# Low parts of weights and norms all subtracted on VectorE instead of every third on GpSimd

## The chip, the cores and the metric

The kernel runs on one core of a Trainium2 chip. Its five engines work in their own order each and wait for each other through semaphores: TensorE (PE in the profile, with its weight load as PEld), VectorE (DVE), ScalarE (ACT), GpSimd (POOL) and SyncE (SP), which here issues the loads. The metric is the device time of one execution in microseconds (us); less is better.

## The reference

The program chains two transformer blocks on a sequence of 256 tokens, width 1024, in fp32. Cut to what matters here:

```python
def first_block(x, ...):
    for layer in range(DEPTH):                       # DEPTH = 2
        h = rms_norm(x, norm1_g[layer])
        sb = cols(SB_OFF, SB_COLS)                   # cols: h @ w_in[layer][:, lo:lo + width]
        y_sb = merge_heads(stick_breaking_attention(...))
        y_rwkv, v_first = rwkv7_time_mix(cols(RWKV_OFF, RWKV_COLS), ...)
        y_moba = merge_heads(moba_attention(q_m, k_m, ...))
        y_hgrn = hgrn2_mixer(...)
        for n, y_n in enumerate((y_sb, y_rwkv, y_moba, y_hgrn)):
            gate = jax.nn.sigmoid(cols(GATE_OFF + n * D_MODEL, D_MODEL))
            term = gate * (y_n @ w_branch[layer, n])
            merged = term if merged is None else merged + term
        x = x + merged @ w_out[layer]
...
def second_block(x, c, ctx, ...):
    mod_l = jax.nn.silu(c) @ w_mod[l] + b_mod[l]
...
    out_c, out_l = mixer(h_c, h_l, ...)              # latent attention and an mLSTM
    x = x + g1[:, None, :] * out_l
    h_l = modulate(rmsnorm(x, norm2[l]), sh2, sc2)
    x = x + g2[:, None, :] * ec_moe(h_l, ...)        # 16 experts
    return rmsnorm(x, final_norm)
```

Behind the mixers each layer of the first block has a norm and an FFN of width 2816, silu(gate) * up, then down. All products are of fp32 quality.

## The kernel before, in words

**How a product is made.** TensorE gets fp32r operands (rounded fp32). To keep the precision, every operand is split into a high part (its copy to fp32r) and a low part (the operand minus that copy). `mm3` (L225) then runs three products into one accumulator: high x high (L227), high weight x low activation (L228) and low weight x high activation (L229), or with the sides exchanged in `proj_tok`.

**Weights.** A pair of halves (`weights`, L219) is the unit of work. `half_weights` (L205) loads one half, 128 x 1024 fp32 (512 KB), on SP's queue into tile wr (L214), ScalarE copies it into wh (`copy`, L179), and the subtraction wr - wh gives wl (`sub`, L182). The pools of wr, wh and wl have four buffers each. A counter `nsplit` sends every third half's subtraction (`NS = 3`, L1969) to GpSimd, the others to VectorE. 349 such halves or parts of halves are subtracted: 234 on VectorE, 115 on GpSimd.

**Norms.** `norm_split` (L335) scales x by the gain and the reciprocal root r (t, L191) and splits the result in high and low, block by block (eight blocks of 128 x 256). In the form without bias, the third and the sixth block's subtraction goes to GpSimd. r comes from a sum of squares (`square_sums` L272 or `rms` L301: products into sm at L280, L285, L309), a short chain of tiny VectorE instructions on tile nr (`rsqrt`, L259), and a spread over the partitions on TensorE (`spread`, L288, L291).

**Other work that the trace names.** VectorE's helpers record one line each: `sub` L182, `add` L185, `mul` L188, `stt` L191 (scalar_tensor_tensor), `ts` L194. In the FFN, `silu_mul` (L1072) makes of a pair of accumulators: u = gate * r, tanh on ScalarE (L1076), t = (t + 1) * u (L191, both inputs in SBUF), u = t * up (L188, `t<-t,acc`, one input in PSUM), u * r on GpSimd (L188, `t<-t,rr`), and the split into ff (L202 on ScalarE, L191 on VectorE, `r<-t,r`). Such GpSimd work that is no low part (the multiplications with rr, some squares and additions in the mixers, masks) is not touched by the change. The mixers run interleaved: `weave` (L867) draws from several streams of emitted work by a table of rates, and waits of TensorE in them carry their lines: L399 (rotation), L415 and L437 (MoBA attention), L642, L674 and L852 (the RWKV recurrence), L1646 (the mLSTM). `modulation` (L1130) loads w_mod in pieces on SP's queue (L1151) between the weight loads and multiplies them at L1155 into wm.

**Order.** The program emits tiles in the order of its loops and of `weave`; the framework's scheduler then fixes one order per engine. Where an instruction is given to another engine, neighbours can change place. The last part, from about 1467 us on, is the mixture of experts, whose weights come as 191 pieces of 1 MB on SP's queue (L1808), used at L1832 and behind.

Of the kernel before, what the change touches and what calls it, by code (L numbers as in the profile page):

```python
# [141 lines left out]
class Block:  # L142
    def __init__(self, ctx, tc, a, out):
        self.ctx, self.tc, self.a, self.out = ctx, tc, a, out
        nc = self.nc = tc.nc
        self.V, self.S, self.G, self.T = nc.vector, nc.scalar, nc.gpsimd, nc.tensor
        e = ctx.enter_context
        self.const = e(tc.tile_pool(name="const", bufs=1))
        self.ps = e(tc.tile_pool(name="ps", bufs=1, space=PSUM))
        self.per = e(tc.tile_pool(name="per", bufs=1))  # L150
        self.cst1 = self.cst2 = None
        self.nsplit = 0


    def C(self, name, lo=0, n=None):
# [49 lines left out]
    def half_weights(self, ap, parts=1):  # L205

        n = ap.shape[1]
        raw = self.wraw.tile([128, 1024], F32, tag="wr", name="wr")[:, 0:n]
        hi = self.whi.tile([128, 1024], F32R, tag="wh", name="wh")[:, 0:n]
        lo = self.wlo.tile([128, 1024], F32R, tag="wl", name="wl")[:, 0:n]  # L210
        self.nsplit += 1
        for i in range(parts):
            c = slice(i * n // parts, (i + 1) * n // parts)
            self.nc.sync.dma_start(raw[:, c], ap[:, c])  # L214
            self.copy(hi[:, c], raw[:, c])
            self.sub(lo[:, c], raw[:, c], hi[:, c], eng=self.G if self.nsplit % NS == 0 else self.V)
        return lambda c, w: (hi[:, c:c + w], lo[:, c:c + w])

    def weights(self, ap, n):  # L219
# [115 lines left out]
    def norm_split(self, x, nk, n, eps, gcol, hi, lo, bias=None, r=None):  # L335

        if r is None:
            r = self.rms8(x) if nk == 8 else self.rms([self.square(x[:, k]) for k in range(nk)], n, eps)
        for k in range(nk):
            h = self.t1()  # L340
            self.stt(h, x[:, k], gcol(k), r, ALU.mult, ALU.mult)
            if bias is None:
                self.split(hi[:, k], lo[:, k], h, eng=self.G if k % 3 == 2 else None)
            else:
                self.S.activation(hi[:, k], h, AF.Identity, bias=bias(k))
                self.stt(lo[:, k], h, bias(k), hi[:, k], ALU.add, ALU.subtract)
# [1619 lines left out]
SMB = 1  # L1966
BV = 1
MS = 0.13
NS = 3  # L1969
FN = 22.3  # L1970
IN = 4.0
GN = 8.2
# [101 lines left out]
```

## Time and profile before

| what | value |
|---|---|
| median of 3 runs | 1900.16 us (1897.15 to 1907.84) |
| the profiled execution | 1902.35 us |
| its span, first to last instruction | 1900.6 us |
| mean granted TensorE clock | 0.931 |
| PE busy | 1691.7 us (89%) |
| DVE busy | 915.7 us (48%) |
| ACT busy | 719.9 us (38%) |
| POOL busy | 454.2 us (24%) |
| read from HBM | 413.63 MB |

Busy times are those of the profiled execution. An engine that is busy is working on an instruction or is held inside one; the profile does not tell these apart. A wait is idle time of an engine, put down to the instruction that released it last. The granted clock is the share of full TensorE speed.

### The profile page before, as it was taken

The page shows a single profiled execution, that of the slowest core. Times are in us where ns is not written, and L with a number is a line of the kernel's source. Part 1 is how long each engine was busy: PE and PEld are TensorE (multiplying, and loading weights), DVE is VectorE, ACT ScalarE, POOL GpSimd, SP SyncE. Part 2 cuts the span into 40 slices and gives each one's busy share as a digit, 9 for nine tenths or more (in the row PEclk, how much of TensorE's full clock was granted, in tenths as well). Part 3 has the DMA queues.
Part 4 walks back from the last instruction along what each step waited for, and adds up shares of the span by engine and source line. Part 5 has one row for each costly group of instructions (what it writes and reads, how often), then busy time and mean ns, then how long its engine had stood idle before and what let it go on. Part 6 is the DMA issues. An engine that isn't in the chain of part 4 may idle for free. (4 is left out here: it accounts for less than half of the span.)

```text
span 1900.6 us, 34082 instructions
## 1 busy us (share of the span) xinstructions
PE 1691.7 (89%) x14380; PEld 1345.7 (71%) x14380; DVE 915.7 (48%) x1395; ACT 719.9 (38%) x1136; POOL 454.2 (24%) x285
## 2 busy tenths in 40 slices
PE   7899899999999799999999999989997976766665
PEld 7668799999989688997998998867896410201113
DVE  8755645577547765553776458453574100000001
ACT  5535544444446455543444444544443300000001
POOL 4352143244323622331443211111231000000000
PEclk9899999999999899999999999989999986767788
DMA  6552546455554235567554553321457999999997
GB/s 225 170 169 96 165 158 190 149 184 172 178 161 155 79 102 185 171 206 238 167 183 143 180 183 130 101 72 65 161 204 301 422 427 427 427 427 427 427 427 320
DMA packets 96378, 416.91 MB, mean 219 GB/s; under 512 B 10688, under 2 KB 12384, under 8 KB 71520
## 3 DMA queue, kind: packets, MB, share of 16 engines
q1 hardware_dynamic: 96224, 414.72, 60.1%
q8 instruction: 113, 1.85, 0.4%
q14 instruction: 41, 0.34, 0.1%
HBM read 413.63 MB, written 1.05 MB: 218 GB/s over the span
## 5 line engine op out<-in xcount | busy, mean ns | idle before, releaser
L227 PE MATMUL acc<-s,wh 128*128 128x256 f32 (+1 forms) x2236 | 652.3, 292 | 11.5 <-ACT wh L179 7.5
L228 PE MATMUL acc<-s,wh 128*128 128x256 f32 (+1 forms) x2236 | 648.0, 290 | 5.3 <-DVE s L191 4.0
L229 PE MATMUL acc<-s,wl 128*128 128x256 f32 (+1 forms) x2236 | 647.8, 290 | 0.4 <-DVE wl L182 0.4
L179 ACT ACTIVATE wh<-wr 128x1024 fp32r<-128x1024 f32 (+2 forms) x349 | 359.4, 1036 | 341.6 <-PE acc L228 201.0
L227 PEld LDWEIGHTS acc<-s,wh 128*128 128x128 f32 x2236 | 436.5, 195 | 28.1 <-issue 15.7
L228 PEld LDWEIGHTS acc<-s,wh 128*128 128x128 f32 x2236 | 436.8, 195 | 15.9 <-issue 7.9
L229 PEld LDWEIGHTS acc<-s,wl 128*128 128x128 f32 x2236 | 436.8, 195 | 4.3 <-issue 1.8
L182 POOL TENSOR_TENSOR wl<-wr,wh 128x1024 fp32r<-128x1024 f32 (+1 forms) x115 | 280.9, 2442 | 660.4 <-ACT wh L179 583.9
L182 DVE TENSOR_TENSOR wl<-wr,wh 128x1024 fp32r<-128x1024 f32 (+2 forms) x234 | 303.9, 1300 | 239.4 <-ACT wh L179 238.3
L1832 PE MATMUL mx<-s,s 128*32 128x512 f32 x640 | 111.7, 788 | 44.4 <-DMA s<-in_w_moe_dram 44.2
L1832 PEld LDWEIGHTS mx<-s,s 128*32 128x32 f32 x640 | 15.6, 121 | 124.4 <-DMA s<-in_w_moe_dram 113.9
L1832 PE MATMUL mx<-mw,s 128*32 128x512 f32 x384 | 68.3, 784 | 26.6 <-DMA mw<-in_w_moe_dram 26.5
L188 POOL TENSOR_TENSOR t<-t,rr 128x256 f32<-128x256 f32 x44 | 42.7, 971 | 127.4 <-DVE t L188 124.7
L1832 PEld LDWEIGHTS mx<-mw,s 128*32 128x32 f32 x384 | 8.8, 121 | 77.1 <-DMA mw<-in_w_moe_dram 67.2
L191 DVE SCALAR_TENSOR_TENSOR x<-acc,mod,x 128x256 f32<-128x256 f32 x28 | 12.2, 479 | 103.4 <-PE acc L1840 100.0
L188 DVE TENSOR_TENSOR m<-m,mx 128x1024 f32<-128x1024 f32 x4 | 4.9, 1221 | 112.0 <-PE mx L1832 112.0
L227 PE MATMUL mx<-r,wh 128*128 128x256 f32 x208 | 58.7, 282 | 0.0
L228 PE MATMUL mx<-r,wh 128*128 128x256 f32 x208 | 58.6, 282 | 0.0
L229 PE MATMUL mx<-r,wl 128*128 128x256 f32 x208 | 58.4, 281 | 0.0
L191 DVE SCALAR_TENSOR_TENSOR m<-m,mx 128x1024 f32<-128x1024 f32 x4 | 4.9, 1219 | 107.0 <-ACT m L1863 107.0
L191 DVE SCALAR_TENSOR_TENSOR t<-t,t 128x256 f32<-128x256 f32 (+1 forms) x46 | 46.8, 1016 | 12.3 <-ACT t L1076 8.2
L1832 PE MATMUL mx<-mw,ht 128*32 128x512 f32 x264 | 39.5, 704 | 14.5 <-DMA mw<-in_w_moe_dram 14.4
(516 smaller groups left out, 2526.5 us busy)
## 6 DMA issues: line engine op xcount, KB each, us to landing
s<-in_w_moe_dram SPq DMA_DIRECT2D x101, 1024.0 KB, 19.6
mw<-in_w_moe_dram SPq DMA_DIRECT2D x90, 1024.0 KB, 19.6
wr<-in_w_in_dram SPq DMA_DIRECT2D x158, 512.0 KB, 3.9
wr<-in_w_gu_dram SPq DMA_DIRECT2D x88, 512.0 KB, 4.3
wr<-in_w_down_dram SPq DMA_DIRECT2D x32, 512.0 KB, 4.3
wr<-in_w_out_dram SPq DMA_DIRECT2D x24, 512.0 KB, 3.8
qk<-in_w_mod_dram SPq DMA_DIRECT2D x32, 256.0 KB, 3.1
wr<-in_w_branch_dram SPq DMA_DIRECT2D x16, 512.0 KB, 4.2
```

The costliest lines, as they stand in the source:

```text
L179: self.S.activation(out, in_, AF.Copy)
L182: (eng or self.V).tensor_tensor(out, a, b, op=ALU.subtract)
L188: (eng or self.V).tensor_tensor(out, a, b, op=ALU.mult)
L191: self.V.scalar_tensor_tensor(out, a, s, b, op0=op0, op1=op1)
L227: T.matmul(out, wh, xh, start=start, stop=False)
L228: T.matmul(out, wh, xl, start=False, stop=False)
L229: T.matmul(out, wl, xh, start=False, stop=stop)
L1832: T.matmul(ps[32 * e:32 * e + 32], lhs(k, e), w[:, e * 512:(e + 1) * 512], start=k == 0, stop=k == 7, tile_position=(0, 32 * e))
```

## The change

`half_weights` gives every low part to VectorE, and `norm_split` as well; the counter and its constant are gone.

```diff
@@ -208,12 +207,11 @@
         lo = self.wlo.tile([128, 1024], F32R, tag="wl", name="wl")[:, 0:n]
-        self.nsplit += 1
         for i in range(parts):
             c = slice(i * n // parts, (i + 1) * n // parts)
             self.nc.sync.dma_start(raw[:, c], ap[:, c])
             self.copy(hi[:, c], raw[:, c])
-            self.sub(lo[:, c], raw[:, c], hi[:, c], eng=self.G if self.nsplit % NS == 0 else self.V)
+            self.sub(lo[:, c], raw[:, c], hi[:, c])
         return lambda c, w: (hi[:, c:c + w], lo[:, c:c + w])
...
@@ -340,7 +338,7 @@
             if bias is None:
-                self.split(hi[:, k], lo[:, k], h, eng=self.G if k % 3 == 2 else None)
+                self.split(hi[:, k], lo[:, k], h, eng=None)
...
-NS = 3
```

115 subtractions of weight halves and five of norms leave GpSimd's order and stand in VectorE's. Lines of the changed kernel are one smaller from L152 on and two smaller from about L211 on (L182 is L181 there, L191 is L190). On TensorE 139 of 11489 matmuls stand elsewhere than before, none by more than 60 places; on SP 7 of 668 instructions.

VectorE, the reciprocal root of the first layer's norm (nr), before:

```order
L194 TENSOR_SCALAR nr<-sm 128x2
L194 TENSOR_SCALAR nr<-nr 128x2
L188 TENSOR_TENSOR nr<-nr 128x2
L191 SCALAR_TENSOR_TENSOR nr<-nr 128x2 x2
L188 TENSOR_TENSOR nr<-nr 128x2 x2
L194 TENSOR_SCALAR nr<-nr 128x2
L191 SCALAR_TENSOR_TENSOR nr<-nr 128x2 x2
L182 TENSOR_TENSOR wl<-wr,wh 128x1024
L188 TENSOR_TENSOR qk<-acc,rr 128x512
```

The same place on VectorE in the changed kernel:

```order
L193 TENSOR_SCALAR nr<-sm 128x2
L181 TENSOR_TENSOR wl<-wr,wh 128x1024
L193 TENSOR_SCALAR nr<-nr 128x2
L187 TENSOR_TENSOR nr<-nr 128x2
L190 SCALAR_TENSOR_TENSOR nr<-nr 128x2
L181 TENSOR_TENSOR wl<-wr,wh 128x1024
L190 SCALAR_TENSOR_TENSOR nr<-nr 128x2
L187 TENSOR_TENSOR nr<-nr 128x2 x2
L193 TENSOR_SCALAR nr<-nr 128x2
L181 TENSOR_TENSOR wl<-wr,wh 128x1024
L190 SCALAR_TENSOR_TENSOR nr<-nr 128x2 x2
L181 TENSOR_TENSOR wl<-wr,wh 128x1024
L187 TENSOR_TENSOR qk<-acc,rr 128x512
```

Three weight subtractions moved from behind or beside the chain into it, so that four stand where one stood.

VectorE, two tiles of the first layer's FFN (t, r and acc as in `silu_mul`; the number is the tile's), before:

```order
L188 TENSOR_TENSOR t_4568<-t_4569,acc 128x256
L182 TENSOR_TENSOR wl<-wr,wh 128x1024
L191 SCALAR_TENSOR_TENSOR r_4071<-t_4568,r_4071 128x256
L188 TENSOR_TENSOR t_4638<-acc,rr 128x256
L191 SCALAR_TENSOR_TENSOR t_4639<-t_4639,t_4638 128x256
L188 TENSOR_TENSOR t_4638<-t_4639,acc 128x256
L191 SCALAR_TENSOR_TENSOR r_4072<-t_4638,r_4072 128x256
L182 TENSOR_TENSOR wl<-wr,wh 128x1024
```

The same place on VectorE in the changed kernel:

```order
L187 TENSOR_TENSOR t_4568<-t_4569,acc 128x256
L181 TENSOR_TENSOR wl<-wr,wh 128x1024
L190 SCALAR_TENSOR_TENSOR r_4071<-t_4568,r_4071 128x256
L187 TENSOR_TENSOR t_4638<-acc,rr 128x256
L181 TENSOR_TENSOR wl<-wr,wh 128x1024
L190 SCALAR_TENSOR_TENSOR t_4639<-t_4639,t_4638 128x256
L187 TENSOR_TENSOR t_4638<-t_4639,acc 128x256
L181 TENSOR_TENSOR wl<-wr,wh 128x1024
L190 SCALAR_TENSOR_TENSOR r_4072<-t_4638,r_4072 128x256
```

In the tile t_4638 one subtraction now stands between the first product and t = (t + 1) * u, and one between the last product and the low part r_4072.

## Rows read from the trace of the kernel before

**Rows 1.** Stretches: from:to, length, busy us (and instructions) by engine, clock, DMA share, GB/s.
```profile
0.00:1467.00 1467.00, 1383.85 (x12432) 1260.37 (x12436) 885.36 (x1334) 686.76 (x1066) 454.18 (x285) 0.97 0.50 162
1467.00:1900.00 433.00, 307.89 (x1952) 85.34 (x1944) 30.39 (x61) 33.16 (x71) 0.00 (x0) 0.79 0.98 412
600.00:650.00 50.00, 41.24 (x437) 35.79 (x435) 45.09 (x53) 29.55 (x48) 21.07 (x12) 0.92 0.35 115
```

**Rows 2.** The page's groups of weight subtractions: busy, mean ns | idle before, releaser.
```profile
L182 POOL TENSOR_TENSOR wl<-wr,wh 128x1024 fp32r<-128x1024 f32 (+1 forms) x115 | 280.9, 2442 | 660.4 <-ACT wh L179 583.9
L182 DVE TENSOR_TENSOR wl<-wr,wh 128x1024 fp32r<-128x1024 f32 (+2 forms) x234 | 303.9, 1300 | 239.4 <-ACT wh L179 238.3
```

**Rows 3.** Timeline, one FFN tile: start, us, engine, line, operation, [idle before <-releaser].
```profile
425.03 2.40 POOL L182 TENSOR_TENSOR wl<-wr,wh 128x1024 fp32r<-128x1024 f32 x1 [1.48 <-ACT wh L179]
425.34 2.37 DVE L191 SCALAR_TENSOR_TENSOR t<-t,t 128x256 f32<-128x256 f32 x1 [0.54 <-ACT t L1076]
428.31 0.36 PE L227 MATMUL acc<-s,wh 128*128 128x256 f32 x1 [0.35 <-DVE t L188]
```

**Rows 4.** Groups by shape of VectorE and GpSimd between 350 and 550 us (FFN).
```profile
L191 DVE SCALAR_TENSOR_TENSOR t<-t,t 128x256 f32<-128x256 f32 x22 | 23.0, 1044 | 4.1 <-ACT t L1076 4.1
L191 DVE SCALAR_TENSOR_TENSOR r<-t,r 128x256 fp32r<-128x256 f32 x13 | 12.5, 960 | 15.1 <-ACT r L202 15.1
L188 DVE TENSOR_TENSOR t<-t,acc 128x256 f32<-128x256 f32 x22 | 9.3, 421 | 0.8
...
L182 POOL TENSOR_TENSOR wl<-wr,wh 128x1024 fp32r<-128x1024 f32 x18 | 43.3, 2406 | 45.0 <-ACT wh L179 23.7 <-PE mx L229 19.9 <-PE acc L228 1.5
```

**Rows 5.** What TensorE waited for: us in total, times, longest us.
```profile
PE wm L1155 <- DMA qk<-in_w_mod_dram: 8.6, 3, 7.6
...
PE sm L642 <- DVE r L191: 4.0, 2, 2.5
PE acc L228 <- DVE s L191: 4.0, 2, 2.0
PE mx L437 <- DVE s L194: 3.6, 3, 3.0
...
PE acc L227 <- DVE t L188: 2.9, 8, 0.4
...
PE sm L309 <- DVE t L185: 2.7, 1, 2.7
PE sm L280 <- ACT t L278: 2.7, 1, 2.7
PE sm L309 <- DVE t L188: 2.5, 1, 2.5
...
PE mx L674 <- DVE s L518: 2.1, 1, 2.1
...
PE sm L399 <- ACT s L179: 1.4, 1, 1.4
...
PE acc L228 <- DVE s L182: 1.1, 1, 1.1
...
PE acc L229 <- DVE wl L182: 0.4, 1, 0.4
```

**Rows 6.** The first of eight stretches at low clock, and the sum of the eight.
```profile
17.00:23.80 6.80, 5.99 (x28) 5.99 (x29) 3.95 (x15) 0.89 (x2) 0.39 (x1) 0.50 0.44 139
...
sum 34.30, PE 33.49 PEld 27.35 DVE 18.62 ACT 7.76 POOL 3.58; mean PE 4.19 PEld 3.42 DVE 2.33 ACT 0.97 POOL 0.45
```

**Rows 7.** Timeline, first layer's mixers at 65 us: GpSimd and VectorE.
```profile
65.20 2.70 POOL L182 TENSOR_TENSOR wl<-wr,wh 128x1024 fp32r<-128x1024 f32 x1
...
66.20 2.25 DVE L182 TENSOR_TENSOR t<-t 128x512 f32<-128x512 f32 x1
```

**Rows 8.** Timeline at 175 us: GpSimd and VectorE.
```profile
175.20 2.36 POOL L182 TENSOR_TENSOR wl<-wr,wh 128x1024 fp32r<-128x1024 f32 x1
...
176.12 0.69 DVE L693 TENSOR_TENSOR am<-mx,cst 128x512 f32<-128x512 f32 x1 [0.44 <-PE mx L691]
```

More of the change, by code (lines that the diff above doesn't have):

```diff
@@ L151, in __init__ @@
         self.cst1 = self.cst2 = None
-        self.nsplit = 0
     def C(self, name, lo=0, n=None):
```

## The prediction

> **What bounds the kernel now.** I read the busy times in two stretches first. Up to 1467 us TensorE is busy for 1383.85 of 1467 us, so it stands still for about 83 us, and neither VectorE (885.36) nor GpSimd (454.18) is full. Behind 1467 us the DMA share is 0.98 at 412 GB/s, and VectorE is busy for 30.39 us, GpSimd for none [rows 1]. That tail is the loading of the experts' weights. It starts when the work before it ends, so a gain before 1467 us should arrive at the end of the program undiminished, and nothing is to be gained behind it.
>
> Second, the low-part subtractions themselves: 234 run on VectorE at 1.30 us, 115 on GpSimd at 2.44 us, and GpSimd waited 583.9 us in front of its own for ScalarE's high copy [rows 2]. So GpSimd has time to spare. What its subtractions cost has to be looked for elsewhere, in what VectorE does beside them.
>
> There it is seen in the timeline of one tile of the first layer's FFN. GpSimd subtracts from 425.03 on for 2.40 us. VectorE's t<-t,t starts at 425.34 and ends with it, after 2.37 us, and TensorE's next tile starts 0.35 us late [rows 3]. The groups of this stage show the pattern: t<-t,t, with both inputs in SBUF, takes 1044 ns on average, while t<-t,acc of the same size, with one input in PSUM, takes 421 [rows 4]. I read this as a hold: a VectorE instruction with two SBUF inputs does not move while a GpSimd subtraction runs.
>
> Third, what stands still because of it: the list of what TensorE waited for. The waits that I connect with a GpSimd subtraction are the two on s (L191), the longest ones of L642 and L437, the eight small ones of the FFN, L309 twice, L280, L674, and five of 1.1 to 1.4 us (L399, L1646, L415, L852 and L228 on L182; first and last are shown) [rows 5]. In each of them a subtraction of GpSimd lies in the chain that releases TensorE. The largest wait, 7.6 us on the load of w_mod, is the end of a load that was issued late, see below.
>
> **The change, part by part.**
>
> *Removed from GpSimd:* 115 weight subtractions, 280.9 us [rows 2], and five of the norms. GpSimd's busy time should fall from 454.18 to about 170.
>
> *Added to VectorE:* 115 x 1.30 + 5 x 0.42 = 152 us. *Given back to VectorE:* in the FFN stage 22 x (1.044 - 0.421) = 13.7 and 13 x (0.960 - 0.421) = 7.0, 20.7 us by 22 subtractions (18 and four narrower ones) [rows 4], or 0.94 each; by 115 of these some 108 us. VectorE's busy time, 915.8, should end between that and 960. So VectorE is about as full as before, with the idle time inside its instructions turned into work.
>
> *Term 1, stops that go.* A hold is worth at most what the row shows, 2.37 - 0.42 = about 2.0 us [rows 3, 4]. With this cap on each stop: L309 2.0 + 2.0, L228 on s 4.0, L642 2.0, L437 2.0, L227 2.9, L280 2.0, L674 2.0, the five small ones 6.2; together 25.1. In some of them something else is late next (ScalarE's own share of the chain, or a hold by one of the instructions that GpSimd keeps), so I take four fifths, **-20.1**. Bounds: 0 and -25.1.
>
> *Term 2, moved subtractions that land in front of something that TensorE waits for.* VectorE works in its order, and the order shows it: in the first norm's chain for the reciprocal root, four subtractions now stand where one stood at the end, so the 2 us that are gained there go back; in the FFN one more stands in every second or third tile between the product and the low part. No row of before prices this as a stop: TensorE's only wait on a wl of VectorE is 0.4 us [rows 5]. Lower bound 0, if all fall into VectorE's idle time. For the upper bound: the 24 stops of term 1 are ends of chains of some 5 us (an estimate; the FFN's piece of it takes 3 us, 425.34 to 428.31), 120 of 1467 us, or one in twelve. If the scheduler puts them where VectorE is busiest it could be one in five: 24 x 1.3 = +31. I take one in twelve of 120, 10 x 1.3, **+13.0**, since the stops are known places and the subtractions are spread like the weights.
>
> *Term 3, the clock.* [...] Most stops only get shorter, and other stops stay, so I take a third, **-5.7**. Bounds: 0 and -17.2.
>
> *Term 4, the late load.* VectorE's subtraction at 66.20 took 2.25 us beside a GpSimd subtraction of 2.70 that began at 65.20 [rows 7]; one of that size takes 0.69 where it is not held [rows 8]. Behind it on VectorE follows a weight subtraction that frees a raw buffer; behind that, on SP's queue, the weight load that needs the buffer, and behind that the w_mod load on which TensorE waits for 7.6 us [rows 5]. The chain starts 2.25 - 0.69 = 1.6 us earlier: **-1.6**. Bounds: 0, and -7.6 if the load gets through before it is needed.
>
> *Costed at nothing:* the weights' own lead. The raw, high and low pools hold four halves each. TensorE waited 0.4 us in all for a low part, so a subtraction that comes 1 or 2 us later or earlier is covered by the halves in hand; without that cover, each would cost its lateness. SP's queue keeps its order but for a few loads at the start that change place with a neighbour.
>
> Sum: -20.1 + 13.0 - 5.7 - 1.6 = **-14.4**. The profiled execution took 1902.35, so 1887.95; the median of the runs, 1900.16, is 2.2 lower, and I say **1887**.
>
> [...] At 176.12 VectorE's am<-mx,cst, with one input in PSUM, took its 0.69 us in the midst of a GpSimd subtraction of 2.36 us that began at 175.20 [rows 8]. [...] There the change buys nothing and only adds 1.3 us each. If all 115 were like this, VectorE would end at 915.8 + 152 = 1068 and term 1 would be nothing; rows 3 and 4 show that they are not.
>
> **The rivals.**
>
> *The insertions take it all back.* Condition: 27.4 us of gain divided by 1.3, 21 subtractions land in front of something TensorE needs, near the upper bound of term 2. For it: between 600 and 650 us VectorE is busy for 45.09 of 50 us [rows 1], with no idle place left. Against it: the hold costs VectorE 0.94 per subtraction and the work 1.3, so even there the engine's load hardly grows. Time: about 1900. [...]
>
> *Slower: subtractions that wait at the head of VectorE's queue.* GpSimd could afford to wait for the high copies, 583.9 us over 115, 5.1 each; VectorE waited 238.3 over 234, 1.0 each [rows 2]. What waits there now keeps the mixers' work behind it. Price: 1.3 + 1.0 = 2.3 for each that sits in front of a chain to TensorE. It decides from 27.4 / 2.3 = 12 of 120; with 18 of them the time is 1902 + 14, **1916**. For it: 83 us of idle TensorE are little, and every new stop may lower the clock too. Against it: the halves are fetched four ahead, so most copies are done early.
>
> *Larger gain.* The clock stays up behind all eight stops and the load comes in time: -20.1 + 13.0 - 17.2 - 7.6 = -31.9, **1870**. For it: clock and stop lie side by side in the rows. Against it: neither the stops nor VectorE's chains go away whole.
>
> That the change does not do what it says can be left out: no low part of a weight is left in GpSimd's order.
>
> **How the numbers follow.** Chances: forecast 0.50 (its own range 1878 to 1896), larger gain 0.12, taken back 0.18, slower 0.20. A measurement of this kernel can tell about 0.5%, 9.5 us, from no change: faster is below 1890.7, which takes seven tenths of the forecast's case and the larger gain, 0.47; the rest of the forecast and the case at 1900 make 0.33; slower 0.20. Range 1868 to 1911: the low end is the larger gain, the high end holds the first part of the slower case and the bound of term 2 (-20.1 + 31 = +11 without clock and load). Outside stay about 0.04 below and 0.12 above.
>
> **What would show it.** Right: POOL busy about 170 us and no wl among its groups; t<-t,t near 0.5 us where it was 1.044; L227 no longer waiting on the FFN's t; DVE busy between 916 and 960; waits on L309, L642, L228 shorter by up to 2 us each; fewer windows at clock 0.50. Wrong: new waits of TensorE on DVE wl or on chains with a wl in them, idle time of DVE before L181 well above 238 us, or TensorE's idle time up to the experts' weights not below 83 us. The tail behind it must stay as long as it is, 433 us; if it shrinks or grows, my account of its bound is wrong.

## The result

The changed kernel takes 1855.16 us (median of 4 runs, 1853.51 to 1857.60), the kernel before in the same comparison 1902.16: a ratio of 0.9753, 95% interval 0.9721 to 0.9785, or 47 us. Faster was forecast, but with 15 us; 1855 lies below the range.

The page of the changed kernel begins with the engines' busy times; of its groups I show the weight subtraction and the one multiplication of the FFN that stays on GpSimd.

```profile
PE 1671.1 (90%) x14380; PEld 1333.6 (72%) x14380; DVE 929.7 (50%) x1515; ACT 725.7 (39%) x1136; POOL 166.1 (9%) x165
...
L181 DVE TENSOR_TENSOR wl<-wr,wh 128x1024 fp32r<-128x1024 f32 (+2 forms) x349 | 425.9, 1222 | 324.3 <-ACT wh L178 323.2
...
L187 POOL TENSOR_TENSOR t<-t,rr 128x256 f32<-128x256 f32 x44 | 32.8, 746 | 353.3 <-DVE t L187 353.3
```

GpSimd lost 288 us and VectorE gained 14: where 115 subtractions of 1.22 us came, nearly as much time in held instructions went. The mean of a subtraction on VectorE fell from 1300 to 1222 ns [rows 2], as some of them had been held themselves (in the kernel before the one at 35.61, beside a GpSimd subtraction of 2.59 us, took 3.42; the median is 1.22).

The same two stretches as before, cut where TensorE stands at the same matmul; the third is the start, where the clock had been at 0.50 [rows 6].

```profile
0.00:1422.00 1422.00, 1368.61 (x12432) 1247.86 (x12436) 899.31 (x1454) 692.67 (x1066) 166.14 (x165) 0.98 0.51 168
1422.00:1855.00 433.00, 302.51 (x1952) 85.69 (x1944) 30.37 (x61) 33.02 (x70) 0.00 (x0) 0.81 0.98 412
17.00:23.80 6.80, 6.80 (x57) 6.73 (x57) 6.51 (x16) 2.33 (x4) 0.00 (x0) 1.00 0.63 216
```

The part with the experts takes 433 us in both, at 412 GB/s in both. All of the gain is in front of it, 45 us in these two executions, and it has two parts: TensorE's idle time fell from 1467 - 1383.85 = 83.2 [rows 1] to 1422 - 1368.61 = 53.4, by 29.8 us; and the same 12432 matmuls kept it busy for 15.2 us less, which goes with the clock: in front of the experts there were 14 stretches at a granted clock of 0.50 and there are 7.

The FFN of the first layer, VectorE's groups by shape between 340 and 535 us:

```profile
L187 DVE TENSOR_TENSOR t<-t,acc 128x256 f32<-128x256 f32 x22 | 9.3, 422 | 0.8
L190 DVE SCALAR_TENSOR_TENSOR t<-t,t 128x256 f32<-128x256 f32 x22 | 9.2, 418 | 0.0
...
L190 DVE SCALAR_TENSOR_TENSOR r<-t,r 128x256 fp32r<-128x256 f32 x13 | 5.4, 418 | 0.0
```

What took 1044 and 960 ns [rows 4] takes 418, as long as the form with one input in PSUM (422).

What TensorE waited for, the lines that answer to those of before, and the two largest that are new or longer:

```profile
PE mx L721 <- POOL am L740: 6.1, 1, 6.1
PE wm L1153 <- DMA qk<-in_w_mod_dram: 5.6, 3, 4.9
...
PE mx L689 <- DVE am L691: 2.2, 1, 2.2
...
PE acc L227 <- DVE wl L181: 1.3, 1, 1.3
...
PE sm L307 <- DVE t L184: 0.9, 1, 0.9
PE mx L435 <- DVE s L193: 0.9, 1, 0.9
...
PE sm L640 <- DVE r L190: 0.4, 1, 0.4
```

Of the waits that term 1 listed [rows 5], the two on s (L191), the FFN's eight, L280, L309's second, L674 in the first layer, L399 and L415 are gone, and those on L309, L437 and L642 are down to under 1 us. Laid side by side by line and by matmul number (in groups of 400), TensorE's idle time was freed at places that add up to 39.5 us, and grew at places that add up to 9.8: (lines of the kernel before) L723, which is L721 now, by 5.0, L691 in the first layer by 2.0, L674 in the second by 1.5, the rest small.

### The profile page after: what moved, and what is told of

It is laid out like the page before. It is cut to its first block, busy times and chain, and to the rows that moved or that the text cites. A ratio compares the mean times of both kernels' runs of the same rounds, so it can differ in the third digit from the quotient of the medians.

```text
span 1855.0 us, 34061 instructions
## 1 busy us (share of the span) xinstructions
PE 1671.1 (90%) x14380; PEld 1333.6 (72%) x14380; DVE 929.7 (50%) x1515; ACT 725.7 (39%) x1136; POOL 166.1 (9%) x165
## 3 DMA queue, kind: packets, MB, share of 16 engines
q8 instruction: 113, 1.85, 0.4%
## 4 chain that ended last, share of the span: by engine, by line
PE 68%; DMA 22%; DVE 5%; ACT 2%; issue 1%; POOL 0%; SPq 0%; DVEq 0%; ACTq 0%; POOLq 0%
PE acc L225 15%; PE acc L226 15%; PE acc L227 15%; DMA s<-in_w_moe_dram 12%; DMA mw<-in_w_moe_dram 10%; PE mx L225 2%; PE mx L226 2%; PE mx L227 2%; PE wm L1153 2%; PE sm L1607 1%; PE mx L721 1%; PE mx L1830 1%; DVE wl L181 1%; PE mx L1574 1%; PE sm L1402 1%
## 5 line engine op out<-in xcount | busy, mean ns | idle before, releaser
L181 DVE TENSOR_TENSOR wl<-wr,wh 128x1024 fp32r<-128x1024 f32 (+2 forms) x349 | 425.9, 1222 | 324.3 <-ACT wh L178 323.2
L227 PEld LDWEIGHTS acc<-s,wl 128*128 128x128 f32 x2236 | 432.4, 193 | 5.6 <-issue 2.1
L187 POOL TENSOR_TENSOR t<-t,rr 128x256 f32<-128x256 f32 x44 | 32.8, 746 | 353.3 <-DVE t L187 353.3
L187 DVE TENSOR_TENSOR m<-m,mx 128x1024 f32<-128x1024 f32 x4 | 4.9, 1222 | 114.7 <-PE mx L1830 114.7
L190 DVE SCALAR_TENSOR_TENSOR x<-acc,mod,x 128x256 f32<-128x256 f32 x28 | 12.2, 479 | 98.9 <-PE acc L1838 95.2
L190 DVE SCALAR_TENSOR_TENSOR m<-m,mx 128x1024 f32<-128x1024 f32 x4 | 4.9, 1220 | 108.5 <-ACT m L1861 108.5
L184 POOL TENSOR_TENSOR s<-s,t 128x512 f32<-128x512 f32 (+1 forms) x24 | 32.9, 1378 | 219.2 <-DVE t L190 219.2
L1861 ACT ACTIVATE m<-mx 128x1024 f32<-128x1024 f32 x4 | 4.1, 1022 | 103.9 <-PE mx L1830 103.9
```

The lines of the kernel that those rows point to most:

```text
L181: (eng or self.V).tensor_tensor(out, a, b, op=ALU.subtract)
L184: (eng or self.V).tensor_tensor(out, a, b, op=ALU.add)
L187: (eng or self.V).tensor_tensor(out, a, b, op=ALU.mult)
L227: T.matmul(out, wl, xh, start=False, stop=stop)
```

## The experiments

Line numbers in the rows of an experiment are those of its own kernel, up to four larger than those of the changed one. The kernel before stood at 1899.77 to 1902.16 us beside these runs, so a difference between two runs that were not taken side by side carries some 2 us.

The theory after the result: the gain is the end of the holds, and it is larger than forecast because the stops had cost the clock as well and because more of them went than I had listed. Its rivals: low parts that are ready earlier (or raw buffers that come free earlier), another order of the instructions, the five subtractions of the norms, and a price of the added subtractions that the sum had too high.

**Only the weights.**

```diff
-                self.split(hi[:, k], lo[:, k], h, eng=None)
+                self.split(hi[:, k], lo[:, k], h, eng=self.G if k % 3 == 2 else None)
```

> Only the 115 weight subtractions move to VectorE; the five subtractions of the norms stay on GpSimd. Theory (GpSimd's subtractions hold VectorE inside its instructions, and TensorE stops behind that): nearly the whole gain is here, 1855 to 1862, since five subtractions of about 0.7 us can hold little. Rival (the norms' subtractions sit at the end of chains that TensorE waits for, so they carry a share out of proportion to their number): 1865 to 1880.

Measured: 1855.42 us, ratio to before 0.9761 (0.9742 to 0.9781). The weights make the whole gain; the norms' part is nothing that can be measured.

**A second, unused subtraction on GpSimd.**

```diff
+        third = self.nsplit % 3 == 0
             self.sub(lo[:, c], raw[:, c], hi[:, c])
+            if third:
+                self.sub(junk[:, c], raw[:, c], hi[:, c], eng=self.G)
```

> All real low parts stay on VectorE as in the changed kernel, but GpSimd makes a second, unused subtraction of every third half into a spare tile (bf16, as there is no room for more). The result is unchanged. Theory (the hold): VectorE's two-input instructions are held again, VectorE has the added work as well, and the time goes back to 1890 to 1910. Rival (the gain came from low parts that are ready earlier, or from another order of instructions): VectorE's low parts are as early as in the changed kernel, so the time stays at 1853 to 1865.

Measured: 1951.24 us, ratio 1.028 (1.0249 to 1.031). The low parts are where the changed kernel has them, and the time is 96 us above it, more than the theory's range. The page's groups, and the FFN's in VectorE's groups between 340 and 600 us:

```profile
L182 POOL TENSOR_TENSOR wj<-wr,wh 128x1024 bf16<-128x1024 f32 (+1 forms) x115 | 349.2, 3037 | 662.9 <-ACT wh L179 429.9 <-issue 212.6 <-DVE r L191 15.6
```

```profile
L191 DVE SCALAR_TENSOR_TENSOR t<-t,t 128x256 f32<-128x256 f32 x22 | 24.5, 1115 | 0.0
```

The holds are back (418 to 1115 ns), and GpSimd's instruction is longer than the subtraction that it stands for (3.04 against 2.44 us), and since its shortest take 2.4 us I read the rest as VectorE holding it in turn. VectorE's 1515 and ScalarE's 1136 instructions stand in the changed kernel's order here, and in the next two runs as well. So neither another order nor the place where the low part is made explains the gain. In one point this run isn't clean: GpSimd's subtraction also keeps the raw tile, which SP's next load needs.

**The same without the raw tile.**

```diff
-                self.sub(junk[:, c], raw[:, c], hi[:, c], eng=self.G)
+                self.sub(junk[:, c], hi[:, c], hi[:, c], eng=self.G)
```

> As the run with a second, unused subtraction on GpSimd, but both of its inputs are the high copy, so the raw tile and with it SP's next weight load are released by VectorE's subtraction alone, as in the changed kernel. If the time of that run (1951) is made by the hold of VectorE: 1935 to 1960 again. If it is made by raw buffers that come free late: 1855 to 1900.

Measured: 1912.25 us, ratio 1.0053 (1.0037 to 1.007). It lies between the two expectations. Most of the 96 us stay (57), but not all. This subtraction takes 2.55 us on average and holds less (t<-t,t at 956 ns). At its shortest it takes 1.89 us, the one with two different tiles 2.35.

Of the other 39 us some 24 go with the shorter holds (161.7 - 114.3 us at 0.50 each, both from the table below); what makes the rest isn't shown. The raw buffers show no share. SP waited for GpSimd's unused subtraction 196 us in the run before this one and not at all here, but TensorE hardly noticed: its waits that end in a weight (w_mod's load, a high copy, a low part) add up to 9.6 + 7.4 + 1.9 = 18.9 us there and 9.6 + 8.4 = 18.0 here. With the real low parts they were 16.5 before and are 13.8 in the changed kernel, so 2.7 us of its gain can come this way. The largest of these waits, in that run and in this one:

```profile
PE wm L1159 <- DMA qk<-in_w_mod_dram: 9.6, 3, 8.4
PE wm L1159 <- DMA qk<-in_w_mod_dram: 9.6, 4, 7.2
```

**An unused instruction with one input on GpSimd.**

```diff
-                self.sub(junk[:, c], hi[:, c], hi[:, c], eng=self.G)
+                self.ts(junk[:, c], hi[:, c], 1.0, None, ALU.mult, ALU.bypass, eng=self.G)
```

> As the last one, but GpSimd's unused instruction has one input (the high copy times one, 128x1024 into the same bf16 tile). If any GpSimd work in SBUF holds VectorE's two-input instructions, the time rises by its length: at 1.2 to 2.4 us each, 1900 to 1950. If only a GpSimd instruction with two inputs does, 1853 to 1865.

Measured: 1875.38 us, ratio 0.9862 (0.9825 to 0.9898). It is the longest of the GpSimd instructions tried (3.52 us on average), and the one that costs least. A tile of the FFN in the timeline, VectorE and GpSimd:

```profile
404.83 3.74 POOL L194 TENSOR_SCALAR wj<-wh 128x1024 bf16<-128x1024 f32 x1
...
405.87 1.25 DVE L191 SCALAR_TENSOR_TENSOR r<-t,r 128x256 fp32r<-128x256 f32 x1
407.04 0.41 DVE L188 TENSOR_TENSOR t<-acc,rr 128x256 f32<-128x256 f32 x1
407.45 1.23 DVE L182 TENSOR_TENSOR wl<-wr,wh 128x1024 fp32r<-128x1024 f32 x1
```

r<-t,r is held for 0.83 us and not for the 2.7 that GpSimd still runs, and behind it a weight subtraction with two SBUF inputs takes its 1.23 us while GpSimd is at work. Both expectations missed: it holds, but not by its length.

One rival stays in part. GpSimd's multiplications with rr stand behind the subtractions in its own order. ScalarE waited for them 100 us in the kernel before and 2.7 in the changed one; it was 117 in the run on the high copy and 35 in this one. What waits there makes r<-t,r late too (VectorE's 15.1 us in the FFN [rows 4]), and no run takes that apart from the hold. That GpSimd is merely occupied does not make the cost: here its unused instructions take 405 us and cost 20, on the high copy 293 and cost 57.

**Every sixth half.**

```diff
-NS = 3
+NS = 6
```

> GpSimd gets every sixth half instead of every third (57 or 58 subtractions), the norms are on VectorE. Theory (each hold costs by itself): about half of the 47 us come back, 1872 to 1884. Rival (a few places, those in the mixers with full VectorE, make the difference): either under 1865 or over 1890, by which of them still have a GpSimd subtraction.

Measured: 1879.55 us, ratio 0.9892 (0.9877 to 0.9907): 24 of the 47 us for half the subtractions, as the theory has it: the cost is spread over the holds and not made in a few places.

**VectorE does it twice.**

```diff
             self.sub(lo[:, c], raw[:, c], hi[:, c])
+            if third:
+                self.sub(junk[:, c], raw[:, c], hi[:, c])
```

> As the changed kernel, but VectorE makes a second, unused subtraction of every third half (115 more, about 140 us more of VectorE, none on GpSimd). It prices what I called term 2. If the prediction's price was right (one in twelve in front of something TensorE needs, 1.3 us each), 1855 + 13 = 1868, at one in five 1886; if VectorE's work of this kind falls into its idle time, 1855 to 1860.

Measured: 1869.33 us, ratio 0.9837 (0.9821 to 0.9852): 14 us for 115 more subtractions, 0.12 us each. VectorE is busy for 1032.63 us up to the experts' part here, as this stretch shows, 133 more than in the changed kernel, with no low part on GpSimd:

```profile
0.00:1434.00 1434.00, 1373.20 (x12432) 1251.31 (x12436) 1032.63 (x1569) 693.52 (x1066) 189.26 (x165) 0.98 0.50 166
```

**No subtraction at all for every third half.**

```diff
+        lo = hi if third else self.wlo.tile([128, 1024], F32R, tag="wl", name="wl")[:, 0:n]
+            if not third:
                 self.sub(lo[:, c], raw[:, c], hi[:, c])
```

> As the changed kernel, but every third half has no subtraction on any engine: its high copy is used as its low part, so the third product of those halves is another one than the reference's. This is the change without the work it adds to VectorE. If the added subtractions cost TensorE something (the prediction's 13 us, and the 14 us that a second set cost in the run that doubles them), 1838 to 1845; if the first 115 fit into idle time and only a second set does not, 1852 to 1857.

Measured: 1846.97 us, ratio 0.9718 (0.9702 to 0.9734), 8.2 us below the changed kernel, between the two expectations. By this the first 115 subtractions cost 8 us and a second set 14, and ending GpSimd's subtractions by itself gave 47 + 8 = 55. The 8 are not VectorE's work alone: without a subtraction the raw tile is free as soon as it is copied.

**Four stops where there were none.**

```diff
         self.S.activation(t, u, AF.Tanh, scale=0.5)
+        for _ in range(10 if slow else 0):
+            self.copy(t, t)
```

> As the changed kernel, but in 4 of the first layer's 22 FFN tiles (j = 3, 8, 13, 18) ScalarE copies the tanh's result onto itself ten times, about 4 us in a chain that has under 2 us to spare; the values stay the same. Four stops of TensorE of 2 to 3 us each, in a stage that runs at full clock without any. If a stop brings a stretch at half clock behind it (theory: that is where 17 us of the gain came from), +8 to +12 for the stops and 4 x 1.7 to 4 x 3.4 for the clock: 1870 to 1880, with granted clock 0.50 behind each. If the clock falls for other reasons, only the stops: 1863 to 1867, clock 1.00 behind them.

Measured: 1875.99 us, ratio 0.9865 (0.9842 to 0.9888), 20.8 above the changed kernel. The wait that it makes, and then the stretch behind each of the four:

```profile
PE acc L225 <- DVE t L187: 14.1, 4, 3.8
```

```profile
374.60:378.00 3.40, 3.27 (x15) 3.30 (x16) 1.23 (x3) 0.83 (x2) 1.42 (x2) 0.50 0.46 154
408.70:412.10 3.40, 3.14 (x15) 3.17 (x16) 1.36 (x4) 0.83 (x2) 1.42 (x2) 0.50 0.43 159
442.80:446.20 3.40, 3.05 (x14) 3.08 (x15) 1.45 (x4) 0.83 (x2) 1.42 (x2) 0.50 0.47 159
477.00:480.40 3.40, 3.09 (x14) 3.12 (x15) 1.41 (x4) 0.83 (x2) 1.43 (x2) 0.50 0.53 161
```

Behind each stop stands one stretch of 3.4 us at 0.50, in a stage that had run at 1.00 throughout. The stops are 14.1 us, longer than I expected, the clock 4 x 1.7 = 6.8, together 20.9: all of the difference. Here the stop is what brings the low clock.

**RWKV's arithmetic off GpSimd, then all of it.** The largest stop of the changed kernel, in its timeline (VectorE, GpSimd and TensorE):

```profile
631.78 1.21 DVE L181 TENSOR_TENSOR wl<-wr,wh 128x1024 fp32r<-128x1024 f32 x1
631.93 2.18 POOL L710 TENSOR_TENSOR am<-am,cst 128x512 f32<-128x512 f32 x1 [1.23 <-DVE am L691]
632.91 1.75 DVE L187 TENSOR_TENSOR t<-qk,t 128x512 f32<-128x512 f32 x1
634.08 1.71 POOL L712 TENSOR_TENSOR am<-am,cst 128x512 f32<-128x512 f32 x1
634.58 2.28 DVE L181 TENSOR_TENSOR wl<-wr,wh 128x1024 fp32r<-128x1024 f32 x1
635.75 2.24 POOL L711 TENSOR_TENSOR am<-am,cst 128x512 f32<-128x512 f32 x1
...
639.62 1.26 POOL L740 TENSOR_TENSOR am<-am,cst 128x512 f32<-128x512 f32 x1
...
640.94 1.86 PE L721 MATMUL mx<-am 64*64 64x64 f32 x29 [6.06 <-POOL am L740]
```

The hold works both ways. VectorE's subtraction from 631.78 to 632.99 holds GpSimd's am, which takes 2.18 us instead of the 1.26 that L740 takes when alone; it ends at 634.1 and has held t<-qk,t until then; and so on, in turn, until TensorE has waited 6 us.

```diff
-        self.mul(kt, kn, eN, eng=G)
+        self.mul(kt, kn, eN)
...
-        G.tensor_tensor(v8(X), v8(ab), mask8("lev1"), op=ALU.mult)
+        V.tensor_tensor(v8(X), v8(ab), mask8("lev1"), op=ALU.mult)
```

> As the changed kernel, and the RWKV mixer's GpSimd arithmetic (L649, L662 to L665, L710 to L713, L740; two inputs in SBUF) is on VectorE too. The largest new stop of the changed kernel is 6.06 us in front of L721, behind five such GpSimd instructions that a VectorE subtraction holds in turn. Theory (either engine holds the other, so one queue without holds is better): this stop shrinks to 2 to 3 us and the time to 1845 to 1853. Rival (VectorE is too full in the mixers): 1856 to 1865.

Measured: 1842.59 us, ratio 0.9698 (0.9679 to 0.9717), a little better than the theory's range. The wait in its list:

```profile
PE mx L721 <- DVE am L740: 3.1, 4, 0.9
```

Where one stop of 6.06 us was, there is none over 0.9. The second step:

```diff
-            self.mul(kt, key, d, eng=self.G)
+            self.mul(kt, key, d)
...
-        self.mul(u, u, r, eng=self.G)
+        self.mul(u, u, r)
```

> As the last one, with HGRN2's multiplication (L513) and the FFN's multiplication by rr (L1075) on VectorE as well. The FFN has no stop left in the changed kernel, so nothing is to be gained there; HGRN2 adds 16 instructions of 0.68 us to the fullest stretch of VectorE. Theory: 0 to 8 us above the last one. Rival (every hold counts, wherever it is): below the last one by 3 to 6 us.

Measured: 1839.68 us, ratio 0.9677 (0.9658 to 0.9696), 2.9 below the last one, by medians; against the last one alone that isn't clear of the spread (1836.59 to 1841.45 against 1841.46 to 1846.47), but no loss, although VectorE has more work. The direction is the rival's. This version beats both kernels, the changed one by 15.5 us.

All of them side by side. "Held" is worked out from each trace: what VectorE's instructions took above the usual duration of their form while a GpSimd subtraction (or the unused instruction in its place) lay over their start; by what is taken as usual it can be 2 us off. Idle and clock are TensorE's, in front of the experts; the clock's loss is the sum of (1 - granted clock) x length.

| kernel | us | held, us (times) | idle, us | lost to clock, us |
|---|---|---|---|---|
| GpSimd twice, raw and high | 1951.24 | 161.7 (99) | 121.5 | 60.2 |
| GpSimd twice, high alone | 1912.25 | 114.3 (81) | 94.5 | 38.8 |
| before | 1902.16 | 118.0 (70) | 83.1 | 40.4 |
| every sixth | 1879.55 | 60.5 (33) | 69.8 | 31.2 |
| four stops | 1875.99 | 0 | 66.5 | 29.8 |
| one input on GpSimd | 1875.38 | 54.4 (83) | 69.4 | 20.9 |
| VectorE twice | 1869.33 | 0 | 60.8 | 27.6 |
| the change | 1855.16 | 0 | 53.4 | 22.9 |
| third without low part | 1846.97 | 0 | 48.3 | 17.3 |
| RWKV off GpSimd | 1842.59 | 0 | 49.1 | 14.4 |
| all off GpSimd | 1839.68 | 0 | 44.4 | 12.2 |

With the added subtractions counted at 8.2 us for 115, a held microsecond costs (47.0 + 8.2) / 118.0 = 0.47 in the kernel before, (24.4 + 4.1) / 60.5 = 0.47 with every sixth, and against the changed kernel 0.50, 0.59 and 0.37 in the runs with unused instructions. So between four and six tenths of what VectorE loses arrives at the end.

## Why the prediction was wrong, by its steps

In front of the experts, 39.5 us of TensorE's idle time went, 9.8 came, and its busy time fell by 15.2: 44.9 where the sum had 14.4. Of the 30.5 that were missing, term 1 makes 16.7, term 3 9.5, term 2 3.2 and term 4 1.1. (A slip besides: 1900.16 - 14.4 is 1885.8, not 1887; nothing hangs on it.)

**Right:** what bounds the kernel, and that a gain in front of the experts arrives whole (433 us of tail in both). The hold as the mechanism: the runs with unused instructions bring it and its cost back with the low parts left where they are. GpSimd at 166 us (170 said), VectorE at 929.7 (916 to 960 said), t<-t,t at 418 ns (near 500 said). The weights' lead, costed at nothing, held too: TensorE waits 1.3 us for a low part, 0.4 before.

**Term 1 was too small.** It said 20.1, and 36.8 went. Three steps failed. The largest is the list of stops itself: some 9 us went at places that I had connected with no GpSimd subtraction, among them L610, L691, L605, a second wait on L280 and 2.0 of the 6.0 on L1536. The second is "so I take four fifths", 5.0 us: at the places of the list 27.8 us of idle time went (1.7 of it the shorter waits on L642 and L437), and what was late next left under 1 us at each. The third is the cap of 2.0 us, with only the longest waits of L642 and L437 under it, 2.7 us in all: L280 lost 2.7, L309's second stop 2.5 and L437 2.3. Why the unlisted places gained is shown for none of them. In front of L280's second wait and of L1609 an instruction of VectorE had been held for 2.1 and 1.85 us, less than 4 us ahead; in the 9 us before L691, L605 and L1536 there was no hold by a low part on GpSimd, so what freed the 4 us there stays open. The load of term 4 gained 2.7 where 1.6 was said.

**Term 2 was about right, in part by luck.** 13.0 us said, 8.2 measured by leaving the subtractions out, 14 for a second set; the places where TensorE's idle time grew add up to 9.8. But 5.0 of these are the stop at L721, which the term did not have: there VectorE's subtractions hold GpSimd's am, besides standing in front of VectorE's own work. The rival "the insertions take it all back" needed 21 subtractions at 1.3 us; the cost is that of 6. One of the term's examples failed: in the first norm's chain nothing goes back. The wait there fell from 2.7 to 0.9 us, and between 17 and 23.8 TensorE is busy for 6.80 of 6.80 us while VectorE, with the four subtractions in the chain, is at 6.51.

**Term 3 was at its bound.** -5.7 said; no run shows that figure, it was my estimate, a third of 17.2, which is half of the 34.30 us in the eight stretches [rows 6]. What the runs showed in its place: TensorE's busy time for the same matmuls fell by 15.2, near the 17.2 that I had kept as the far end. The step that failed is "Most stops only get shorter, and other stops stay, so I take a third". All eight stretches are gone, and their stops were either gone or down to 0.9 us. One new one of 6.8 us came, at 102.4, behind the new stop of 2.2 us on L691. In the table the clock's loss is between 0.27 and 0.50 of the idle time, mostly more where that is longer. The four added stops show the cause: 14.1 us of stops carried 6.8 of clock with them. A stop in this kernel cost up to half as much again, and the right sum for term 3 would have been made with term 1 and not apart from it.

**The rival on the other side** did not come about. VectorE waits 323.2 us in front of 349 subtractions, 0.93 each, where it was 238.3 over 234, 1.0 each [rows 2]: the high copies are no later than they were. I had named this idle time as a sign that I was wrong; as a sum it grew, by the number of the subtractions, and meant nothing. The sign should have been given for a single subtraction.

**The larger gain** (1870) had both terms in it and would have been nearer, still 15 us short, for it kept term 1 at four fifths.

## What to carry to other kernels

Add up what the waiting engine loses inside its instructions, by comparing one form held and not held, and price the sum (here half a microsecond for each held one) instead of listing only the stops whose chain one has followed: here the list was not whole. Price TensorE's stops with the clock stretch behind them, as one term (here 14.1 us of added stops carried 6.8 of clock). Here VectorE paid for work with two SBUF inputs on GpSimd, 118.0 us in 70 holds; with a third of its time free, the same work on VectorE cost 0.07 to 0.12 us for each subtraction of 1.2 us.

## What the runs showed of the hardware

The hold is mutual: beside VectorE's subtractions GpSimd's am took 2.18 and 2.24 us in the changed kernel, alone 1.26.

GpSimd's instruction with one input held VectorE least though it is the longest: 54.4 us in 83 holds, 0.66 each, at 3.52 us on average; the subtraction of one tile from itself 1.41 each at 2.55, the one with two different tiles 1.63 each at 3.04. Beside GpSimd's subtraction VectorE's t<-t,t took 2.37 us [rows 3], where it takes 0.42 in the changed kernel; under GpSimd's instruction with one input VectorE's subtraction at 407.45 ran through in its 1.23 us. What lets it through isn't settled here.
